# W_down of a decoder layer as seven products of quarters, with the quarter sums formed behind gate and up

## The chip, the cores and the metric

One core of a Trainium2 chip runs the whole program. The metric is the device time of one execution in microseconds; lower is better. A core has a matrix engine (TensorE; PE in the rows, PEld its weight loads), VectorE (DVE), ScalarE (ACT), GpSimd (POOL) and SyncE (SP), which issues most of the transfers. Each engine takes its own instructions in order and waits for the others by semaphores. Tiles lie in SBUF, products come out in PSUM, inputs and outputs lie in device memory (DRAM).

## What is computed

One layer of a hybrid decoder over 512 tokens of 1024 features, in float32: a gated short convolution and a sparse attention, merged by gates, then a SwiGLU feed-forward part and a final RMSNorm. The end, where the change lies, is this:

```
    h = h + mix @ w_o                                      # mix: 512 x 1024
    n = rmsnorm(h, g_ffn)
    h = h + (silu(n @ w_gate) * (n @ w_up)) @ w_down       # 512x1024 @ 1024x2816, 512x2816 @ 2816x1024
    return rmsnorm(h, g_final)
```

## The kernel before

**Splitting.** A matmul of float32 is made of three: each operand is split into a rounded part H (type float32r) and a remainder L, and `mm` (lines 117 to 121) adds H*H, H*L and L*H into one PSUM bank. A weight chunk, 128 x 1024, goes through `wchunk` (line 105): `load` puts it into `raw` by a transfer on SyncE's queue, `split` (line 92) copies it on ScalarE into `wh` (line 95) and subtracts on VectorE or GpSimd into `wl` (line 96). The pool `wp` has three buffers of each. In the matmul rows the names behind the arrow are the moving operand, then the stationary one.

**Order.** TensorE's instructions stand in the order of the source (`manual_schedule`); those of the other engines are put in order by a scheduler. Transfers on one queue are issued in their order, and one that waits holds up those behind it.

**Stages.** Projections, compressed keys, and an attention over 32 units with other products as filler take the first 430 us, with the output projection of the attention and W_o behind them until 526 us. Then, in `trace`:

- *Gate and up* (lines 909 to 936). For each of 22 feature tiles (`FT`) of 128 rows, `dense` multiplies a chunk of W_gate, then one of W_up, with the normalised tokens nH/nL (moving, 512 columns, 24 matmuls each). `ffn_act` (line 918) makes the activation: silu on ScalarE, the product on VectorE (line 921), then the split into `aH` and `aL` (lines 922, 923). The first three chunks are split early, into parts of aH/aL that are still free (`early_chunk`, line 857).
- *W_down* (lines 938 to 1009). Stationary is the activation, moving the chunk of W_down. First the left 512 output columns for all four token tiles, chunk by chunk, then the right 512, whose last token tile is cut into two halves of 256 columns. `wd_mm` is the inner product:

```
        for ff in range(2):
            k = 2 * fc + ff
            c = slice(ff * 512 + c0, ff * 512 + c0 + n)
            mm(ps, (aH[:, k, ts_], aL[:, k, ts_]), (w[0][:, c], w[1][:, c]),
               k == 0, k == FT - 1)
...
    for fc in range(NF):
        w = wchunk(a["wd"][0, fc], eng=nc.vector)
        for t in range(NT):
            wd_mm(pss[t], w, fc, t, 0, 512)
```

- *The end* (`add_sq`, `var`, `scale_out`, lines 946 to 1010). The PSUM tile is added into the residual `h1`, squared with a row sum on ScalarE, made into a power -0.5 on GpSimd; then `h1` is scaled and written out per token tile.

**Addresses.** SBUF tiles are placed one behind the other at multiples of 32 bytes. In the built program nH, nL, wh and wl begin at multiples of 128 bytes, aH and aL 96 bytes past one, yH and yL 32 past, oH, oL, q, th and tl 64 past.

Of the kernel before, what the change touches and what calls it, by code (L numbers as in the profile page):

```python
# [51 lines left out]
def trace(tc, a):  # L52
# [12 lines left out]
    gmix = const([P, KD], "gmix")  # L65
    convw = const([P, 4, 3], "convw")
# [453 lines left out]
    def expo(u, h):  # L520
        pr, i = units[u]
        if h == 0:
            U[u]["sm"] = ap_.tile([P, 2, 3], F32, name="sm", bufs=3)
        pt, nm = U[u]["pts"][h], U[u]["nms"][h]
        for b in range(3):
            s = U[u]["pc"][:, h] if b == 0 else pt[:, (b - 1) * S:(b - 1) * S + U[u]["w"]]
            nc.scalar.activation(s, s, AF.Exp,  # L527
                                 scale=-1.0, bias=nm[:, b:b + 1],
                                 accum_out=U[u]["sm"][:, h, b:b + 1])

    def norm(u):
        pr, i = units[u]
        fac = ap_.tile([P, 2, 3], F32, name="fac")
# [383 lines left out]

    def ffn_act(ft, pg, pu):
        sg = fp.tile([P, S], F32, name="sg", bufs=2)
        nc.scalar.activation(sg, pg, AF.Silu)  # L920
        nc.vector.tensor_tensor(sg, pu, sg, op=ALU.mult)  # L921
        nc.scalar.activation(aH[:, ft], sg, AF.Copy)
        nc.vector.tensor_tensor(aL[:, ft], sg, f(aH[:, ft]), op=ALU.subtract)

    ffn_act(0, pp[0], pp[1])
    for ft in range(1, FT):
        if ft == 1:
# [8 lines left out]
        ffn_act(ft, pg, pu)  # L936

    def wd_mm(ps, w, fc, t, c0, n):
        ts_ = slice(t * P, (t + 1) * P)
        for ff in range(2):  # L940
            k = 2 * fc + ff
            c = slice(ff * 512 + c0, ff * 512 + c0 + n)
            mm(ps, (aH[:, k, ts_], aL[:, k, ts_]), (w[0][:, c], w[1][:, c]),
               k == 0, k == FT - 1)

    def add_sq(ps, t, cs, q):
        nc.vector.tensor_tensor(h1[:, t, cs], ps, h1[:, t, cs], op=ALU.add)
# [9 lines left out]
    NF = FT // 2  # L957
    half = slice(0, 512)
    pss = [acc.tile([P, S], F32, name="acc") for _ in range(NT)]
    for fc in range(NF):  # L960
        w = wchunk(a["wd"][0, fc], eng=nc.vector)
        for t in range(NT):
            wd_mm(pss[t], w, fc, t, 0, 512)
    for t in range(NT):
        add_sq(pss[t], t, half, 0)
        var(t, 0, EPS)
        nc.gpsimd.tensor_tensor(h1[:, t, half], h1[:, t, half], gfin[:, half], op=ALU.mult)  # L967


    parts = [(t, 0, 512) for t in range(3)] + [(3, 0, 256), (3, 256, 256)]  # L970
    pss = [acc.tile([P, S], F32, name="acc") for _ in parts]

    def part(i, ws, f0):
        t, c0, n = parts[i]
        for q, w in enumerate(ws):
            wd_mm(pss[i][:, 0:n], w, f0 + q, t, c0, n)

    for fc in range(NF - 2):
        w = wchunk(a["wd"][1, fc], eng=nc.vector)
        for i in range(5 if fc < NF - 3 else 3):  # L980
            part(i, [w], fc)
    ws = [w] + [wchunk(a["wd"][1, fc], eng=nc.vector) for fc in range(NF - 2, NF)]

    rest = slice(512, D)

    def scale_out(t):
        r = st[:, t, 1:2]
        lo, hi = h1[:, t, half], h1[:, t, rest]
# [4 lines left out]
        (nc.scalar if t == 0 else nc.sync).dma_start(a["out_0"][t][:, half], lo)
        nc.vector.scalar_tensor_tensor(hi, in0=hi, scalar=r, in1=gfin[:, rest],
                                       op0=ALU.mult, op1=ALU.mult)
        nc.sync.dma_start(a["out_0"][t][:, rest], hi)

    for i, (t, c0, n) in enumerate(parts):
        if i < 3:
            part(i, ws[1:], NF - 2)  # L1000
        else:
            part(i, ws, NF - 3)
        q = 1 if i < 4 else 2
        add_sq(pss[i][:, 0:n], t, slice(512 + c0, 512 + c0 + n), q)
        if i in (1, 2, 4):
            scale_out(t - 1)
        var(t, q, st[:, t, 0:1])
        if i != 3:
            nc.gpsimd.tensor_tensor(st[:, t, 1:2], st[:, t, 0:1], mhalf[:, 0:1], op=ALU.pow)
    scale_out(3)  # L1010
# [3 lines left out]
def layout(inp):  # L1014
# [69 lines left out]
```

## Time and profile before

| | us |
|---|---|
| median of three runs (913.68 to 916.31) | 913.7 |
| the profiled execution | 913.92 |
| its span, first to last instruction | 912.1 |
| gate and up | 547.8 to 781.2 |
| W_down | 781.2 to 905.0 |
| after the last matmul | 7.1 |

The rows further down are of the profiled execution. Times in them count from its first instruction. A matmul's row lasts until its result is out, longer than the distance to the next one: how fast they follow each other is read from their starts. "Idle before" is the time that the engine stood still, with what ended it.

### The profile page before, as it was taken

The numbers are of one execution on the slowest core, as the hardware profiler recorded it, in microseconds if no ns is written. First come the engines' busy times: TensorE is split into PE (matmuls) and PEld (weight loads), VectorE is DVE, ScalarE is ACT, GpSimd is POOL, SyncE is SP. The second block draws the span as 40 slices with busy tenths as digits, with TensorE's granted clock in tenths as the row PEclk, the third lists the DMA queues.
The fourth block names the chain that finished last, engine by engine and source line by source line (L and its number), as shares of the span: only waits on it lengthen the run. The fifth ranks groups of instructions, "written<-read, shape, count | busy, mean of one in ns | idle before, by whom it ended". The sixth has DMA issues, their size and how long they took to land.

```text
span 912.1 us, 12767 instructions
## 1 busy us (share of the span) xinstructions
PE 892.1 (98%) x4757; PEld 761.3 (83%) x4757; DVE 518.0 (57%) x1219; ACT 425.0 (47%) x936; POOL 119.1 (13%) x79
## 2 busy tenths in 40 slices
PE   8989899999999999999999999999999999999996
PEld 7789788888888888888889999888888888888885
DVE  4896788888888888765456442333333333223223
ACT  6345686767767777664323522222233222212212
POOL 1000423233242222330000300000000000001100
PEclk9999999999999999999999999999999999999999
DMA  8235511211212121124434700233333233323312
GB/s 308 76 114 157 173 47 47 57 61 48 69 47 71 46 64 54 58 65 163 154 93 131 216 2 24 93 93 101 106 94 93 93 98 108 94 93 93 93 47 92
DMA packets 26269, 85.14 MB, mean 93 GB/s; under 512 B 3424, under 2 KB 3680, under 8 KB 26208
## 3 DMA queue, kind: packets, MB, share of 16 engines
q1 hardware_dynamic: 24912, 82.78, 28.9%
q10 hardware_dynamic: 1296, 1.55, 0.5%
q8 instruction: 37, 0.61, 0.3%
q14 instruction: 24, 0.20, 0.1%
HBM read 82.23 MB, written 2.10 MB: 92 GB/s over the span
## 4 chain that ended last, share of the span: by engine, by line
PE 89%; DVE 6%; ACT 3%; issue 1%; DMA 1%; POOL 0%; POOLq 0%; ACTq 0%; DVEq 0%
PE acc L119 24%; PE acc L120 24%; PE acc L121 24%; PE sc L500 4%; PE tp L568 4%; PE av L587 2%; PE av L586 2%; DVE blk L249 2%; PE sc L119 1%; PE sc L121 1%; PE sc L120 1%; ACT wh L95 1%; PE av L581 1%; DVE wl L96 1%; DMA raw<-wq 1%
## 5 line engine op out<-in xcount | busy, mean ns | idle before, releaser
L95 ACT ACTIVATE wh<-raw 128x1024 fp32r<-128x1024 f32 (+2 forms) x143 | 144.5, 1012 | 317.4 <-PE acc L120 116.0
L119 PE MATMUL acc<-nH,wh 128*128 128x512 f32 x656 | 262.7, 400 | 0.0
L121 PE MATMUL acc<-nH,wl 128*128 128x512 f32 x656 | 256.4, 391 | 1.1 <-POOL wl L96 1.1
L120 PE MATMUL acc<-nL,wh 128*128 128x512 f32 x656 | 256.3, 391 | 0.0
L96 DVE TENSOR_TENSOR wl<-raw,wh 128x1024 fp32r<-128x1024 f32 (+2 forms) x107 | 123.8, 1158 | 170.2 <-ACT wh L95 169.9
L121 PEld LDWEIGHTS acc<-nH,wl 128*128 128x128 f32 x656 | 123.2, 188 | 27.7 <-POOL wl L96 1.5
L119 PEld LDWEIGHTS acc<-nH,wh 128*128 128x128 f32 x656 | 123.5, 188 | 21.4
L120 PEld LDWEIGHTS acc<-nL,wh 128*128 128x128 f32 x656 | 123.6, 188 | 21.3
L96 POOL TENSOR_TENSOR wl<-raw,wh 128x1024 fp32r<-128x1024 f32 x36 | 86.2, 2399 | 232.9 <-ACT wh L95 91.1
L121 PE MATMUL acc<-wh,aL 128*128 128x512 f32 (+1 forms) x198 | 73.5, 371 | 0.0
L119 PE MATMUL acc<-wh,aH 128*128 128x512 f32 (+1 forms) x198 | 73.4, 371 | 0.0
L120 PE MATMUL acc<-wl,aH 128*128 128x512 f32 (+1 forms) x198 | 73.4, 371 | 0.0
L527 ACT ACTIVATE pt<-pt,nm 128x128 f32<-128x128 f32 (+3 forms) x128 | 70.7, 554 | 3.6 <-DVE nm L512 2.9
L512 DVE CUSTOM_DVE_ANT_0 pt<-sc,tri,nrs 128x128 f32<-128x128 f32 (+3 forms) x128 | 65.4, 547 | 0.1
L572 DVE TENSOR_TENSOR tl<-tp,th 128x512 fp32r<-128x512 f32 x80 | 55.2, 690 | 11.6 <-ACT th L571 9.8
L921 DVE TENSOR_TENSOR sg<-acc,sg 128x512 f32<-128x512 f32 x22 | 15.2, 692 | 80.7 <-PE acc L121 80.7
L571 ACT ACTIVATE th<-tp 128x512 fp32r<-128x512 f32 x80 | 47.3, 592 | 10.2 <-PE tp L568 9.3
L568 PE MATMUL tp<-ident,pt 128*128 128x128 f32 x320 | 48.3, 273 | 0.1
L967 POOL TENSOR_TENSOR h<-h,gfin 128x512 f32<-128x512 f32 x4 | 6.0, 1536 | 299.1 <-ACT jk L949 299.1
L120 PEld LDWEIGHTS acc<-wl,aH 128*128 128x128 f32 x198 | 37.3, 189 | 7.1
L119 PEld LDWEIGHTS acc<-wh,aH 128*128 128x128 f32 x198 | 37.3, 189 | 7.1
L121 PEld LDWEIGHTS acc<-wh,aL 128*128 128x128 f32 x198 | 37.3, 188 | 7.0
(231 smaller groups left out, 1503.8 us busy)
## 6 DMA issues: line engine op xcount, KB each, us to landing
raw<-wg SPq DMA_DIRECT2D x22, 512.0 KB, 3.5
raw<-wu SPq DMA_DIRECT2D x22, 512.0 KB, 3.5
raw<-wd SPq DMA_DIRECT2D x22, 512.0 KB, 3.5
raw<-wcv SPq DMA_DIRECT2D x12, 512.0 KB, 3.5
raw<-wq SPq DMA_DIRECT2D x8, 512.0 KB, 3.5
raw<-w SPq DMA_DIRECT2D x8, 512.0 KB, 3.5
raw<-wgc SPq DMA_DIRECT2D x8, 512.0 KB, 3.5
raw<-wga SPq DMA_DIRECT2D x8, 512.0 KB, 3.4
```

Source lines behind the costliest of these rows:

```text
L95: nc.scalar.activation(h[:, :n], raw[:, :n], AF.Copy)
L96: ins = (eng or nc.gpsimd).tensor_tensor(l[:, :n], raw[:, :n], f(h[:, :n]), op=ALU.subtract)
L119: nc.tensor.matmul(ps, lhs[0], rhs[0], start=first, stop=False)
L120: nc.tensor.matmul(ps, lhs[0], rhs[1], start=False, stop=False)
L121: nc.tensor.matmul(ps, lhs[1], rhs[0], start=False, stop=last)
L249: nc.vector.tensor_tensor(blk[lp * HD:(lp + 1) * HD, :, 2 * ct + hp, 0:NB - 1], src, pos, op=ALU.add)
L500: nc.tensor.matmul(o, q[:, h, qs], kk[g // 2][:, g % 2, c0:c0 + n], start=(j == 0), stop=(j == 1))
L512: nc.vector.tensor_tensor_reduce(out=pt[:, r0:r0 + w].rearrange("p (j c) -> p j c", c=P), in0=sv[:, b], in1=tri[:, NT - 1 - i:NT], scale=n ...
L527: nc.scalar.activation(s, s, AF.Exp, scale=-1.0, bias=nm[:, b:b + 1], accum_out=U[u]["sm"][:, h, b:b + 1])
L568: nc.tensor.transpose(tp[:, (2 * b + h) * P:(2 * b + h + 1) * P], pts[h][:, r0:r0 + P], ident)
L571: nc.scalar.activation(th, tp, AF.Copy)
L572: nc.vector.tensor_tensor(tl, tp, f(th), op=ALU.subtract)
```

## The change

With the activation A (512 x 2816) and W_down each cut into 2 x 2 quarters (256 x 1408 and 1408 x 512), the four quarters of the result come from seven products of quarters in place of eight; the operands of most are sums or differences of quarters. Row tiles: 2 per product, inner tiles: 11 (`NK`), 512 columns.

- *Weight sums.* Five sums or differences of quarters of W_down are formed once per inner tile, during feature tiles 2 to 12 of gate and up: `sums_load` fetches four pieces of 128 x 512 into the staging tiles of name `n2`, `sums` makes five results on VectorE (tied behind the newest activation product by a dependency for the scheduler) and writes them to a DRAM tile `scr`. Loads and stores are all on SyncE's queue.
- *Activations.* `ffn_act` now keeps the product in `a_`, in full, and for the first 11 feature tiles splits the operands of products 0 and 1 at once into `aC`, which has two slots. `prep_a` makes the operand of product i + 1 while product i runs, a difference of two quarters first where one is needed.
- *The product stage.* 42 chunks (six per product, the sixth of half width) are loaded three ahead, from `scr` or `wd`, into the `raw`, `wh` and `wl` buffers in turn. From the fourth on their split parts go into quarter slots of nH and nL, which then are the moving operands. Each product's two PSUM tiles are added to, or subtracted from, one or two quarters of `h1`. Token tiles 2 and 3 are complete after product 5 and written out then; the last product, in two halves of 256 columns for its second row tile, completes tiles 0 and 1.
- *Early chunks* get a pool of their own (`eyp`) for H, and parts of `aC` for L.
- *Even addresses.* Small constants share the tiles `few` and `rfew`; `uu`, `ssq` and `st` are padded; `sm` and `fac` get four buffers. In the built program nH, nL, wh, wl, a_, aC, yH, yL, oH, oL, q, th and tl all begin at multiples of 128 bytes.

The core of the diff:

```diff
-    gmix = const([P, KD], "gmix")
-    convw = const([P, 4, 3], "convw")
+
+    few = const([P, 32], "few")
+    gmix, rstd, warm = few[:, 0:8], few[:, 8:12], few[:, 12:13]
+    rfew = pool(es, name="rbase", bufs=1, side="right").tile([P, 24], F32, name="rfew")
+    convw = rfew[:, 0:12].rearrange("p (m j) -> p m j", j=3)
+    mhalf, nrs8, nrs = [rfew[:, i:i + NT] for i in (12, 16, 20)]
...
-            u = oyp.tile([P, S + 2], F32, name="uu")
+            u = oyp.tile([P, S + 32], F32, name="uu")[:, 0:S + 2]
...
-    aH = fp.tile([P, FT, S], F32R, name="aH")
-    aL = fp.tile([P, FT, S], F32R, name="aL")
+
+    NK = FT // 2
+    eyst = ExitStack()
+    eyp = pool(eyst, name="eyp", bufs=1, side="right", reuse_waits="tile")
+    aC = fp.tile([P, 2, 2, NK, 256], F32R, name="aC")
+    aCf = aC.rearrange("p s e k c -> p (s e k c)")
     early = []
 
     def early_chunk(src, eng):
         q = len(early)
-        r = slice(FT - 2 * q - 2, FT - 2 * q)
         raw = load(src, 1024)
-        h, l = [t[:, r].rearrange("p f s -> p (f s)") for t in (aH, aL)]
+        h = eyp.tile([P, 1024], F32R, name=f"ey{q}")
+        l = aCf[:, (10 - q) * 1024:(11 - q) * 1024]
...
         sg = fp.tile([P, S], F32, name="sg", bufs=2)
         nc.scalar.activation(sg, pg, AF.Silu)
-        nc.vector.tensor_tensor(sg, pu, sg, op=ALU.mult)
-        nc.scalar.activation(aH[:, ft], sg, AF.Copy)
-        nc.vector.tensor_tensor(aL[:, ft], sg, f(aH[:, ft]), op=ALU.subtract)
+        a = a_[:, ft]
+        ins = nc.vector.tensor_tensor(a, pu, sg, op=ALU.mult)
+        prods.append((ins.ins if hasattr(ins, "ins") else ins).name)
+        if ft < NK:
+            part_a(0, ft, 1, a[:, lo])
+            d = fp.tile([P, S], F32, name="sg", bufs=2)[:, lo]
+            nc.vector.tensor_tensor(d, a[:, hi], a[:, lo], op=ALU.subtract)
+            part_a(1, ft, 1, d)
+
+    def part_a(s, k, n, src):
+        h, l = [aC[:, s, e, k:k + n].rearrange("p k c -> p (k c)") for e in range(2)]
+        nc.scalar.activation(h, src, AF.Copy)
+        nc.vector.tensor_tensor(l, src, f(h), op=ALU.subtract)
...
+    def sums_load(k):
+        for i in range(4):
+            nc.sync.dma_start(quart[i], a["wd"][i // 2, i % 2][:, k * 512:(k + 1) * 512])
+
+    def sums(k):
+        cs = slice(k * 512, (k + 1) * 512)
+        o = [gffn[:, 0:512], gffn[:, 512:D]]
+        b11, b12, b21, b22 = quart
+        for n, out, x, y in (("11+12", o[0], b11, b12), ("12+22", b12, b12, b22),
+                             ("11-22", o[1], b11, b22), ("11+21", b11, b11, b21),
+                             ("21+22", b22, b21, b22)):
+            ins = nc.vector.tensor_tensor(out, x, y,
+                                          op=ALU.subtract if "-" in n else ALU.add)
+
+            tc.add_manual_dep(ins.ins if hasattr(ins, "ins") else ins, prods[-1],
+                              mybir.DependencyInfo(mybir.DependencyClass.Sync,
+                                                   mybir.DependencyReason.SCHED_ONLY))
+            nc.sync.dma_start(scr[SUMS[n]][:, cs], out)
...
+        if 2 <= ft < 2 + NK:
+            sums_load(ft - 2)
...
+    PRODS = [((0, 0), None, "12+22", [(0, 1, 1), (1, 1, 1)]),
+             ((1, 0), (0, 0), "11+12", [(1, 1, 1)]),
+             ((1, 1), (1, 0), "11", [(1, 0, -1), (1, 1, 1)]),
+             ((0, 1), (0, 0), "22", [(0, 1, 1), (0, 0, -1)]),
+             ((0, 0), (1, 1), "11-22", [(0, 0, 1), (1, 1, 1)]),
+             ((1, 1), None, "11+21", [(0, 0, 1), (1, 0, 1)]),
+             ((0, 1), (1, 1), "21+22", [(0, 0, 1)])]
+    NQ = (NK + 1) // 2
+    chunks = [(i, q) for i in range(len(PRODS)) for q in range(NQ)]
+    wq_ = {}
+
+    def prep_w(n):
+        if n >= len(chunks):
+            return
+        i, q = chunks[n]
+        b = PRODS[i][2]
+        w = 512 * min(2, NK - 2 * q)
+        src = scr[SUMS[b]] if b in SUMS else a["wd"][int(b[0]) - 1, int(b[1]) - 1]
+        src = src[:, q * 1024:q * 1024 + w]
+        if n < 3:
+            wq_[n] = wchunk(src, w, nc.vector)
+            return
+        nm = ("raw", "wh", "wl")[n % 3]
+        raw = wp.tile([P, 1024], F32 if nm == "raw" else F32R, name=nm)
+        raw = raw if nm == "raw" else f(raw)
+        nc.sync.dma_start(raw[:, :w], src)
+        r = slice(2 * (n % 4), 2 * (n % 4) + 2)
+        h, l = [t[:, r].rearrange("p k c -> p (k c)") for t in (nH, nL)]
+        nc.scalar.activation(h[:, :w], raw[:, :w], AF.Copy)
+        nc.vector.tensor_tensor(l[:, :w], raw[:, :w], f(h[:, :w]), op=ALU.subtract)
+        wq_[n] = h, l
...
+        k, n = 4 * piece, min(4, NK - 4 * piece)
+        (r, g), m = PRODS[i][0], PRODS[i][1]
+        x = a_[:, g * NK + k:g * NK + k + n, TH[r]]
+        if m is not None:
+            d = fp.tile([P, D], F32, name="n2", bufs=2)[:, 0:n * 256]
+            d = d.rearrange("p (k c) -> p k c", c=256)
+            nc.vector.tensor_tensor(d, x, a_[:, m[1] * NK + k:m[1] * NK + k + n, TH[m[0]]],
+                                    op=ALU.subtract)
+            x = d
+        h, l = [aC[:, i % 2, e, k:k + n] for e in range(2)]
+        nc.scalar.activation(h, x, AF.Copy)
+        nc.vector.tensor_tensor(l, x, f(h), op=ALU.subtract)
...
+    AHEAD = 3
+    for n in range(AHEAD):
+        prep_w(n)
+    for i in range(len(PRODS)):
+        last = i == len(PRODS) - 1
+        pss = [acc.tile([P, S], F32, name="acc") for _ in (PARTS if last else PARTS2)]
+        for q in range(NQ - 3 if last else NQ):
+            n = i * NQ + q
+            prep_w(n + AHEAD)
+            for ps, (u, c0, c1, _) in zip(pss, PARTS if last else PARTS2):
+                wd_mm(ps, n, u, c0, c1)
+            if q % 2:
+                prep_a(i + 1, q // 2)
+        if last:
+            break
+        for u in range(2):
+            for r, c, sign in PRODS[i][3]:
+                evac(pss[u], u, r, c, sign)
...
+            elif i == 5:
+                square(2 + u, CH[0], 1)
+                var(2 + u, 1, st[:, 2 + u, 0:1])
+                rpow(2 + u)
+                scale_out(2 + u)
+
+    for ps, (u, c0, c1, q) in zip(pss, PARTS):
+        for n in range(len(chunks) - 3, len(chunks)):
+            wd_mm(ps, n, u, c0, c1)
```

**Two places where the order changes.** First SyncE's queue in gate and up; `raw` is a weight chunk's buffer, n_6071 and n_6072 are the two staging tiles, gffn holds two of the five results. Before, pairs of wg and wu follow each other with nothing between them, up to the last pair, the chunks of W_down and the outputs:

```order
L89 DMA raw<-wg 128x1024
L89 DMA raw<-wu 128x1024
L89 DMA raw<-wd 128x1024 x22
L996 DMA out<-h_5317 128x512
L993 DMA out<-h_5317 128x512
```

With the change, from one pair in the middle of gate and up to the next:

```order
L88 DMA raw<-wg 128x1024
L88 DMA raw<-wu 128x1024
L973 DMA scr<-gffn 128x512 x2
L973 DMA scr<-n_6071 128x512 x2
L973 DMA scr<-n_6072 128x512
L958 DMA n_6072<-wd 128x512
L958 DMA n_6071<-wd 128x512 x2
L958 DMA n_6072<-wd 128x512
L88 DMA raw<-wg 128x1024
L88 DMA raw<-wu 128x1024
```

Between two pairs of weight chunks there now stand five stores of sums and four loads of the next pieces.

Second VectorE in the W_down stage. Before, from the end of gate and up through the left half of the output (line 96 the splits of weight chunks, line 947 the additions into h1):

```order
L921 TENSOR_TENSOR sg<-acc,sg 128x512
L96 TENSOR_TENSOR wl<-raw,wh 128x1024
L923 TENSOR_TENSOR aL<-sg,aH 128x512
L96 TENSOR_TENSOR wl<-raw,wh 128x1024 x10
L947 TENSOR_TENSOR h_5317<-acc,h_5317 128x512 x2
L954 TENSOR_SCALAR st<-ssq 128x1
```

With the change, between the additions of product 1 and those of product 2 (line 1034 makes differences of activation quarters, n_7950 to n_8216; line 1039 their remainders; line 1022 splits weight chunks):

```order
L1022 TENSOR_TENSOR nL<-raw,nH 128x1024
L1022 TENSOR_TENSOR nL<-wh,nH 128x1024
L1039 TENSOR_TENSOR aC<-n_7950,aC 128x768
L1022 TENSOR_TENSOR nL<-wl,nH 128x512
L1039 TENSOR_TENSOR aC<-n_7992,aC 128x1024
L1034 TENSOR_TENSOR n_8028<-a 128x1024
L1034 TENSOR_TENSOR n_8058<-a 128x768
L1022 TENSOR_TENSOR nL<-raw,nH 128x1024
L1039 TENSOR_TENSOR aC<-n_8028,aC 128x1024
L1022 TENSOR_TENSOR nL<-wh,nH 128x1024
L1034 TENSOR_TENSOR n_8216<-a 128x1024
L1022 TENSOR_TENSOR nL<-wl,nH 128x1024
```

Where splits of weight chunks stood alone, they now alternate with differences and remainders of activations.

## Rows read from the trace of the kernel before

**Rows 1.** The page: busy time per engine, and the chain that ended last.

```profile
PE 892.1 (98%) x4757; PEld 761.3 (83%) x4757; DVE 518.0 (57%) x1219; ACT 425.0 (47%) x936; POOL 119.1 (13%) x79
...
PE 89%; DVE 6%; ACT 3%; issue 1%; DMA 1%; POOL 0%; POOLq 0%; ACTq 0%; DVEq 0%
```

**Rows 2.** Windows: length, busy time and count per engine, granted clock, DMA share, GB/s.

```profile
547.80:781.20 233.40, 233.40 (x1074) 195.17 (x1073) 76.86 (x83) 66.18 (x85) 0.00 (x0) 1.00 0.30 91
781.20:905.00 123.80, 123.77 (x594) 102.47 (x593) 34.77 (x41) 28.18 (x39) 7.64 (x7) 1.00 0.26 81
905.00:912.10 7.10, 0.00 (x0) 0.00 (x0) 1.65 (x5) 1.34 (x5) 0.54 (x1) 0.83 0.39 148
```

**Rows 3.** Timeline, TensorE, gate and up, then W_down: start, us, engine, line, operation.

```profile
600.14 0.39 PE L119 MATMUL acc<-nH,wh 128*128 128x512 f32 x1
...
700.11 0.39 PE L119 MATMUL acc<-nH,wh 128*128 128x512 f32 x1
...
781.03 0.39 PE L119 MATMUL acc<-wh,aH 128*128 128x512 f32 x1
...
847.09 0.28 PE L119 MATMUL acc<-wh,aH 128*128 128x256 f32 x1
...
848.50 0.40 PE L119 MATMUL acc<-wh,aH 128*128 128x512 f32 x1
```

**Rows 4.** Timeline, TensorE: six matmuls with oH/oL, ten of W_o with nH/nL.

```profile
459.86 0.39 PE L119 MATMUL acc<-oH,wh 128*128 128x512 f32 x1
...
461.24 0.39 PE L119 MATMUL acc<-oH,wh 128*128 128x512 f32 x1
...
493.97 0.28 PE L119 MATMUL acc<-wh,nH 128*128 128x256 f32 x1
...
495.17 0.28 PE L120 MATMUL acc<-wl,nH 128*128 128x256 f32 x1
```

**Rows 5.** Groups of instructions by form, VectorE and ScalarE: busy us, mean ns, idle before.

```profile
L96 DVE TENSOR_TENSOR wl<-raw,wh 128x1024 fp32r<-128x1024 f32 x91 | 112.5, 1236 | 167.4 <-ACT wh L95 167.2
...
L96 DVE TENSOR_TENSOR wl<-raw,wh 128x512 fp32r<-128x512 f32 x8 | 5.5, 686 | 0.9 <-ACT wh L95 0.9
...
L947 DVE TENSOR_TENSOR h<-acc,h 128x512 f32<-128x512 f32 x7 | 4.7, 687 | 5.7 <-PE acc L121 5.7
...
L947 DVE TENSOR_TENSOR h<-acc,h 128x256 f32<-128x256 f32 x2 | 0.8, 416 | 0.0
...
L95 ACT ACTIVATE wh<-raw 128x1024 fp32r<-128x1024 f32 x127 | 134.2, 1058 | 304.8 <-PE acc L120 108.7 <-issue 97.2 <-PE acc L121 81.2
```

**Rows 6.** DMA issues: KB each, us to landing; then xT's and out's landing.

```profile
raw<-wd SPq DMA_DIRECT2D x22, 512.0 KB, 3.5
...
xT<-xT SPq DMA_DIRECT2D x8, 256.0 KB, 4.5
...
DMA to landing us min/median/max: 2.7/4.5/6.6
...
DMA to landing us min/median/max: 2.0/2.3/2.8
```

**Rows 7.** Windows in which the DMA engines were full; the last figure is GB/s.

```profile
9.00:12.00 3.00, 3.00 (x15) 2.46 (x14) 1.20 (x2) 0.63 (x1) 0.00 (x0) 1.00 1.03 342
...
432.00:436.00 4.00, 4.00 (x20) 3.30 (x19) 2.82 (x4) 1.00 (x2) 0.00 (x0) 1.00 1.00 364
```

**Rows 8.** Timeline, VectorE, gate and up.

```profile
640.71 1.23 DVE L96 TENSOR_TENSOR wl<-raw,wh 128x1024 fp32r<-128x1024 f32 x1 [0.16 <-ACT wh L95]
...
646.14 1.23 DVE L96 TENSOR_TENSOR wl<-raw,wh 128x1024 fp32r<-128x1024 f32 x1 [3.61 <-ACT wh L95]
```

**Rows 9.** Timeline, the end: last matmul, last addition, last output.

```profile
904.70 0.28 PE L121 MATMUL acc<-wh,aL 128*128 128x256 f32 x1
...
905.27 0.41 DVE L947 TENSOR_TENSOR h<-acc,h 128x256 f32<-128x256 f32 x1
...
908.43 0.38 SPq L996 DMA_DIRECT2D out<-h  x1
```

More of the change, by code (lines that the diff above doesn't have):

```diff
@@ L532, in norm @@
         pr, i = units[u]
-        fac = ap_.tile([P, 2, 3], F32, name="fac")
+        fac = ap_.tile([P, 2, 3], F32, name="fac", bufs=4)
         gv = gates[:, i].rearrange("p (b h) -> p h b", h=HEADS)[:, 2 * pr:2 * pr + 2]
@@ L916, in trace @@
     dense(pp[2][:, hi], wgu[2], nH, nL, cols=hi)
+    FH = (slice(0, NK), slice(NK, FT))
+    TH = (lo, hi)
+    SUMS = {"12+22": 0, "11+12": 1, "11+21": 2, "11-22": 3, "21+22": 4}
+    sd = pool(es, name="sd", bufs=1, space=bass.MemoryType.DRAM)
+    scr = sd.tile([5, P, NK * 512], F32, name="scr")
+    eyst.close()
+    fq = pool(es, name="fq", bufs=1, side="right", reuse_waits="tile")
+    a_ = fq.tile([P, FT, S], F32, name="a")
     def ffn_act(ft, pg, pu):
@@ L936, in trace @@
         ffn_act(ft, pg, pu)
[L938 to L947, printed above, removed]
+        if 2 <= ft < 2 + NK:
+            sums(ft - 2)
@@ new lines, in prep_a @@
+    def prep_a(i, piece):
+        if not 2 <= i < len(PRODS):
+            return
+        k, n = 4 * piece, min(4, NK - 4 * piece)
[10 more added lines that the diff above has]
+        nc.vector.tensor_tensor(l, x, f(h), op=ALU.subtract)
@@ L948, in add_sq, with wd_mm, square @@
+    def wd_mm(ps, n, u, c0, c1):
+        i, q = chunks[n]
+        w = wq_[n]
+        for kk in range(min(2, NK - 2 * q)):
+            k = 2 * q + kk
+            at = [aC[:, i % 2, e, k, u * P:(u + 1) * P] for e in range(2)]
+            c = slice(kk * 512 + c0, kk * 512 + c1)
+            mm(ps[:, c0:c1], at, (w[0][:, c], w[1][:, c]), k == 0, k == NK - 1)
+    def square(t, cs, q):
         jk = lp.tile([P, S], F32, name="jk", bufs=2)
@@ L955, in var @@
                                 op0=ALU.mult, op1=ALU.add)
[L957 to L984, printed above, removed]
+    def rpow(t):
+        nc.gpsimd.tensor_tensor(st[:, t, 1:2], st[:, t, 0:1], mhalf[:, 0:1], op=ALU.pow)
@@ L995, in scale_out @@
+        nc.vector.scalar_tensor_tensor(y, in0=y, scalar=r, in1=gfin[:, CH[0]],
                                        op0=ALU.mult, op1=ALU.mult)
[L996 to L1009, printed above, removed]
@@ L1011, in trace @@
+    for ps, (u, c0, c1, q) in zip(pss, PARTS):
+        for n in range(len(chunks) - 3, len(chunks)):
+            wd_mm(ps, n, u, c0, c1)
+        cs = slice(c0, c1)
+        nc.vector.tensor_tensor(h1[:, u, cs], h1[:, u, cs], ps[:, cs], op=ALU.add)
+        square(u, cs, q)
+        if q == 1 and u == 1:
+            scale_out(0)
+        var(u, q, st[:, u, 0:1])
+        if (u, q) != (1, 1):
+            rpow(u)
+    scale_out(1)
     es.close()
```

50 lines of the change are left out of this document (32 added, 18 removed).

## The prediction

> **What bounds the kernel now.** First the page's busy shares and its chain of waits [rows 1]: TensorE is busy 98% of a 912.1 us span and holds 89% of the chain, so time is won only where TensorE has less to do or is fed sooner. The window table by stage [rows 2] then shows where this change works. Gate and up (547.8 to 781.2) keep TensorE busy without a gap with VectorE at 77 of 233 us and the DMA engines 30% busy at 91 GB/s; W_down (781.2 to 905.0) is 123.8 us of TensorE with VectorE at 35; a tail of 7.1 us follows in which TensorE does nothing. The granted clock is 1.00, the 2.4 GHz level, in both stages.
>
> How long a matmul takes is read from the distance of starts, since the durations of the rows overlap. In gate and up 441 matmuls of 512 columns lie between 600.14 and 700.11: 226.7 ns each. In W_down the 282 of 512 columns from 781.03 to 847.09 take 234.3 ns, the 12 half-width ones after them 117.5 [rows 3]. Nothing waits between them. The stage is 462 full and 132 half matmuls, 594 in the table's count, and 462 x 234.3 + 132 x 117.7 ns is its 123.8 us.
>
> **The change, part by part.**
>
> *The products.* Seven products of quarters, each 2 x 11 x 3 = 66 matmuls of 512 columns, are 462 in place of 528 full-width equivalents; as the order of the changed program shows, 429 stand at full width and 66 at half (the last product's second row tile). What each costs is the open point. The changed program moves nH/nL slices over stationary aC, both tiles at multiples of 128 bytes, where aH/aL began 96 bytes past one. Low end: the spacing of gate and up, whose moving operand is the same nH/nL: 429 x 226.7 + 66 x 113.3 = 104.7 us. High end: W_down's present spacing: 429 x 234.3 + 66 x 117.7 = 108.3 us. Rows do not say that the address decides: the products with oH start 64 bytes past a multiple of 128 and are spaced 230 ns, but W_o's first half has both operands at such multiples and is spaced 120.0 ns at 256 columns [rows 4], above the 113.3 that half of 226.7 would be. I take 230 ns, between the ends and equal to the oH row, and 116.5 for the halves: 98.7 + 7.7 = 106.4 us. **-17.4 us**, ends -15.5 and -19.1.
>
> By the Trainium skill (TensorE: Matmul & The Clock Gate, Back-to-back issue gap) the warm spacing follows from the columns alone, 215.7 ns at 512. By it 66 fewer matmuls save 14.2 us (an estimate) and addresses nothing; both spacings of the trace lie above it, so I use the rows.
>
> *Other tiles at even addresses.* In the built program 96 products with yH/yL, 192 with oH/oL, 256 with q, 320 with th/tl and 144 of the first gate and up products had an operand off a multiple of 128: 1,008. At nothing each (the W_o rows) to about 4 ns (half of W_down's 7.6, most being narrower) that is 0 to -4.0 us; **-1.2 us**, near the W_o end, because attention also waits for other engines.
>
> *Weight chunks and row-block operands in the product stage.* Per chunk ScalarE has one copy of 1.06 us and VectorE one subtraction of 1.24; a half chunk 0.69 [rows 5]; I take a 768-wide one at 0.96, between them. Per product VectorE gets five chunks and a half chunk (6.9 us), the remainders of the next product's left operand (2 x 1.24 + 0.96 = 3.4), in four products their differences before that (3.4), and two or four additions into h1 at 0.69 (1.4 or 2.8). TensorE needs 66 x 0.230 = 15.2. Products 2 and 3 have everything: 16.5, so VectorE falls 1.3 us behind in each. Over the stage it has 44.4 + 17.2 + 11.3 + 15.1 = 88 us before the last product's own additions, against 106, and it may be up to three chunks of 2.8 us ahead, since four slots of nH/nL take turns. In product 0 the list is 14.3 and in product 1 15.1, so some lead survives. **+0.5 us**, ends 0 and +2.6 (no lead). Chunk 4 is the tightest load: its buffer is chunk 0's, free 2.8 us into the stage, and 3.5 to landing [rows 6] plus 1.06 and 1.24 makes 8.6, where TensorE wants it at 11.0. ScalarE's 8.9 us per product are covered.
>
> *Quarter sums.* Over eleven feature tiles of 10.9 us each (two products of 24 x 0.2267) come 5 additions of 0.69 on VectorE, 3.4 us, so its load is 0.69 + 3 x 0.42 + 2 x 1.24 + 3.4 = 7.8 of 10.9: covered. On SP come four loads and five stores of 256 KB per tile, and wg and wu of a later tile stand behind them: 11 issues of about 0.33 us. The loop that must close within 10.9 us runs from the last sum: its store 0.35 + 2.3 to landing, the load that takes its place 0.35 + 4.5 (xT's median, same size, taken while the engines were full), four sums 2.8: 10.3 us. By bytes a tile moves 1.05 of weights + 1.05 + 1.31 = 3.41 MB; full engines moved 342 to 364 GB/s [rows 7], so 9.4 to 10.0 us. Both fit, barely: **0**, at the upper ends a loss (rival B). The cover if they don't fit: a split may start when a weight buffer frees, two chunks (10.9 us) before its use, as the splits 5.43 us apart show [rows 8]; 2.3 of that is its own work, and sums that stand ahead of it on VectorE take some 1.3 more, so about 7 us of lag cost TensorE nothing.
>
> *The tail.* From the last matmul's start (904.70) to the end the same add, square, power and scaling follow [rows 9]; rows 256 to 511 leave a product earlier: 0, within 0.5. Tiles for constants, padding and two more buffers of sm and fac: nothing waited for them.
>
> **Sum.** -17.4 - 1.2 + 0.5 = -18.1 on the profiled execution's 913.9 us (its span and 1.8 around it): 895.8. The median of the runs is 0.2 lower: **895.6 us**.
>
> **Rivals.**
>
> A: *addresses change nothing.* Spacing stays 234.3: -15.5 + 0.5, so 898.7 us. For: W_o's rows. Against: gate and up run at 226.7 with the same moving tile. The skill's rule above is this case told more strictly and would give about 900.
>
> A': *both tiles do reach 226.7 and the other products profit*: -19.1 and up to -4.0, 890.6 to 893.
>
> B, *the other side: the quarter loop does not close.* SP takes its queue in order; if a store lands late, the load behind it, the sums, and then wg and wu all slip, and VectorE stands before a load with the next splits behind it. With a loop of L us the lag is 11 x (L - 10.9), less the 7 covered. At L = 12 TensorE loses 5 us (900.6), at L = 13.2 it loses 18 and the whole gain is gone: that is the turning point. The slowest rows, 2.8 for a store and 6.6 for a load, give 0.35 + 2.8 + 0.35 + 6.6 + 2.8 = 12.9, 15 us lost: 910.6. Against: those 6.6 were seen at the start, where several loads were issued at once. The skill (DMA: Bandwidth & Descriptors, Latency and other measured facts) has HBM access at 0.2 us on average and 2 under high load. With 1.8 more on each landing the loop would be about 13.9 (an estimate), some 26 us lost; this trace, with stores only at the end, cannot show it.
>
> C: *VectorE binds products 2 to 5* without any lead: +2.6, 897.7 us.
>
> D: *the change does not do what it says*: fewer matmuls are certain from the order (4,658 against 4,757), so this could only be that another wait takes their place at 781, at most 0.02.
>
> **How the numbers follow.** Forecast 0.38; A' 0.17; A 0.18; C 0.08; B between 11.6 and 13.2 us of loop 0.11; B beyond 0.06; D 0.02. A measurement of this kernel tells about 0.3%, 2.7 us, from no change. Everything but B's upper part and D is faster by more: 0.92. Same 0.02 (B close to its turning point or D), slower 0.06. The range goes from A' to B at a loop of 12.2: 890.5 to 903; left out are 0.04 below, and above it B's rest, 0.14.
>
> **What would show it.** Right: 4,658 matmuls; TensorE without gaps from 547 to the end of the products; the stage some 106 us; spacing of acc<-nH,aC between 226.7 and 234.3, which settles A, A' and the forecast by itself; DMA in gate and up near 300 GB/s with VectorE 70% busy until the thirteenth tile. Wrong: TensorE idle before gate and up products released by wl's subtraction or a load (B), or idle inside products 2 to 5 released by VectorE's nL or aC (C); a distance of the sums above 10.9 us in gate and up (B).

## The result and the profile after

The changed kernel takes **897.5 us** (median of four runs, 896.9 to 898.8) where the kernel before took 914.1 beside it: ratio 0.9816, 95% interval 0.980 to 0.9832. Forecast were 895.6, within 890.5 to 903. The profiled execution has a span of 895.9 us, 16.2 less than before.

The page of the changed kernel, busy time and chain, against [rows 1]:

```profile
PE 875.3 (98%) x4658; PEld 746.5 (83%) x4658; DVE 607.9 (68%) x1349; ACT 451.0 (50%) x970; POOL 118.3 (13%) x77
...
PE 85%; DVE 7%; ACT 3%; DMA 2%; issue 1%; SPq 0%; POOL 0%; POOLq 0%; ACTq 0%; DVEq 0%
```

TensorE is still busy 98%, with 4,658 matmuls; VectorE has gone from 57 to 68%. The windows of gate and up, of the products and of the tail (columns as in [rows 2]):

```profile
548.20:781.50 233.30, 233.30 (x1073) 194.92 (x1072) 110.83 (x152) 62.86 (x86) 0.00 (x0) 1.00 0.60 200
781.50:889.10 107.60, 107.60 (x496) 88.56 (x494) 89.35 (x102) 58.02 (x72) 6.71 (x5) 1.00 0.53 174
889.10:895.90 6.80, 0.07 (x1) 0.00 (x0) 1.51 (x4) 1.31 (x4) 0.54 (x1) 0.83 0.40 154
```

Gate and up take the 233.3 us that they took, though VectorE's time rose from 77 to 111 and the traffic from 91 to 200 GB/s. The products take 107.6 in place of 123.8, TensorE never idle in them. That is nearly all: from the first product's start to the last one's start 107.42 us against 123.67 (-16.25); the first product starts 0.45 later (781.48 against 781.03); from the last start to the end 6.97 in place of 7.41 (-0.44). Together -16.24.

The timeline of TensorE gives the spacing in the new stage; between these two rows lie 308 matmuls of 512 columns:

```profile
796.82 0.39 PE L118 MATMUL acc<-nH,aC 128*128 128x512 f32 x1
...
868.39 0.39 PE L120 MATMUL acc<-nH,aC 128*128 128x512 f32 x1
```

71.57 us / 308 = **232.4 ns**. [Rows 3] have 234.3 in W_down and 226.7 in gate and up; 230 was forecast. The starts repeat every 21 matmuls to the nanosecond (228 to 241 ns). Rows have whole nanoseconds; but for 1 to 2 ns it is every 7, as in W_down before, while in gate and up nearly every distance is 226 or 227 ns. A PSUM tile takes six matmuls of a chunk, and 7 fits no buffer's turn here. That speaks for the stream of operands itself as what sets the spacing; the first experiments test it.

The quarter sums did not run as forecast. VectorE's timeline around the last of the eleven, and the product that needs the split behind it:

```profile
684.62 1.23 DVE L95 TENSOR_TENSOR wl<-raw,wh 128x1024 fp32r<-128x1024 f32 x1
691.82 0.69 DVE L967 TENSOR_TENSOR gffn<-n 128x512 f32<-128x512 f32 x1 [5.98 <-DMA n<-wd]
...
694.85 1.22 DVE L95 TENSOR_TENSOR wl<-raw,wh 128x1024 fp32r<-128x1024 f32 x1
...
700.32 0.39 PE L120 MATMUL acc<-nH,wl 128*128 128x512 f32 x1
```

VectorE stands 6 us before a load of a quarter, and the split behind the sums is done at 696.07, 4.26 us before its use. When the sums are over, this lead is 9.04: a split at 733.58 ends at 734.80 and is used at 743.84. From the second feature tile with sums on, the first additions start at 588.77, 599.66, 610.54, 621.41, 632.29, 643.17 (10.88 apart, TensorE's pace), then at 654.46, 665.64, 678.68 and 691.82: 11.3, 11.2, 13.0 and 13.1 apart, 5.1 us behind in the end. The page has the median landing times behind it:

```profile
n<-wd SPq DMA_DIRECT2D x44, 256.0 KB, 3.7
scr<-n SPq DMA_DIRECT2D x33, 256.0 KB, 4.2
...
scr<-gffn SPq DMA_DIRECT2D x22, 256.0 KB, 4.3
```

### The profile page after: what moved, and what is told of

It reads as the page before. It is cut to its first block, busy times and chain, and to the rows that moved or that the text cites. A ratio compares the mean times of both kernels' runs of the same rounds, so it can differ in the third digit from the quotient of the medians.

```text
span 895.9 us, 12997 instructions
## 1 busy us (share of the span) xinstructions
PE 875.3 (98%) x4658; PEld 746.5 (83%) x4658; DVE 607.9 (68%) x1349; ACT 451.0 (50%) x970; POOL 118.3 (13%) x77
## 4 chain that ended last, share of the span: by engine, by line
PE 85%; DVE 7%; ACT 3%; DMA 2%; issue 1%; SPq 0%; POOL 0%; POOLq 0%; ACTq 0%; DVEq 0%
PE acc L118 23%; PE acc L120 23%; PE acc L119 23%; PE sc L499 4%; PE tp L567 4%; PE av L586 2%; PE av L585 2%; DVE blk L248 2%; DVE wl L95 1%; ACT wh L94 1%; PE av L580 1%; DMA w2kr<-w2k 1%; DMA raw<-wk 1%; DMA xT<-xT 0%; DMA xt<-x 0%
## 5 line engine op out<-in xcount | busy, mean ns | idle before, releaser
L94 ACT ACTIVATE wh<-raw 128x1024 fp32r<-128x1024 f32 (+2 forms) x124 | 124.3, 1005 | 239.2 <-PE acc L119 188.6
L95 DVE TENSOR_TENSOR wl<-raw,wh 128x1024 fp32r<-128x1024 f32 (+2 forms) x88 | 100.0, 1138 | 53.2 <-ACT wh L94 52.3
L120 PE MATMUL acc<-nH,aC 128*128 128x512 f32 (+1 forms) x201 | 71.4, 355 | 0.0
L511 DVE CUSTOM_DVE_ANT_0 pt<-sc,tri,rfew 128x128 f32<-128x128 f32 (+3 forms) x128 | 65.4, 545 | 0.1
L938 DVE TENSOR_TENSOR a<-acc,sg 128x512 f32<-128x512 f32 x22 | 15.2, 691 | 70.2 <-PE acc L120 60.4
L119 PE MATMUL acc<-nL,aC 128*128 128x512 f32 (+1 forms) x153 | 57.9, 378 | 0.0
L118 PE MATMUL acc<-nH,aC 128*128 128x512 f32 (+1 forms) x153 | 57.9, 378 | 0.0
L570 ACT ACTIVATE th<-tp 128x512 fp32r<-128x512 f32 x80 | 47.3, 592 | 10.3 <-PE tp L567 9.5
L526 ACT ACTIVATE pc<-pc,nm 128x32 f32<-128x32 f32 x64 | 20.5, 320 | 47.1 <-DVE nm L506 46.9
L1108 POOL TENSOR_TENSOR h<-h,gfin 128x512 f32<-128x512 f32 x2 | 3.4, 1701 | 302.5 <-ACT jk L1052 302.5
L542 DVE TENSOR_SCALAR pt<-pt,fac 128x128 f32<-128x128 f32 (+3 forms) x128 | 42.8, 379 | 0.0
L120 PEld LDWEIGHTS acc<-nH,aC 128*128 128x128 f32 x201 | 37.8, 188 | 5.8
```

The lines of the kernel that those rows point to most:

```text
L94: nc.scalar.activation(h[:, :n], raw[:, :n], AF.Copy)
L95: ins = (eng or nc.gpsimd).tensor_tensor(l[:, :n], raw[:, :n], f(h[:, :n]), op=ALU.subtract)
L118: nc.tensor.matmul(ps, lhs[0], rhs[0], start=first, stop=False)
L119: nc.tensor.matmul(ps, lhs[0], rhs[1], start=False, stop=False)
L120: nc.tensor.matmul(ps, lhs[1], rhs[0], start=False, stop=last)
L511: nc.vector.tensor_tensor_reduce(out=pt[:, r0:r0 + w].rearrange("p (j c) -> p j c", c=P), in0=sv[:, b], in1=tri[:, NT - 1 - i:NT], scale=n ...
```

## The experiments

Three questions were open: what sets the spacing, what the sums cost and how near they are to binding, and how near VectorE is. Medians are beside the kernel before on the same chip, whose median was 915.9 us for the first group of runs, 914.5 for the second and 915.6 for the third, so ratios count rather than microseconds. Stage lengths and spacings agree between profiles of the same stage within 0.01 us and 0.1 ns (107.42 us in five of them), so the stages carry the argument and the whole times only go along with it.

**What sets the spacing.** In the built program nH, nL, wh and wl begin at the same place modulo 512 bytes, before and after; aC begins 384 past them, aH and aL began 352 past. The first group moves aC, with the tiles `ey` and `a_` that lie below it; in the product stage aC is the only matmul operand of these:

```
-    aC = fp.tile([P, 2, 2, NK, 256], F32R, name="aC")
-    aCf = aC.rearrange("p s e k c -> p (s e k c)")
+    aCf = fp.tile([P, 4 * NK * 256 + PAD], F32R, name="aC")[:, 0:4 * NK * 256]
+    aC = aCf.rearrange("p (s e k c) -> p s e k c", s=2, e=2, k=NK)
```

with PAD 96, 32, 8 and, later, 16; a larger PAD puts aC lower by four bytes for each element.

*aC 0 past (PAD 96).* 

> The changed kernel with aC (and ey and a_ below it) 384 bytes lower, so that aC begins at a multiple of 512 bytes as nH, nL, wh and wl do; nothing else is moved. In the changed kernel aC begins 384 past such a multiple, and its products stand 232.4 ns apart, with a strict period of 21 matmuls. Theory (distance): what sets the spacing is the distance of the stationary operand's address from the moving one's, modulo 256 or 512; at 0 (gate and up: 226.7 ns) it is shortest. Then 226.7 at 512 columns, the stage 429 x 0.2267 + 66 x 0.119 = 105.1 us in place of 107.4, the kernel 895.1 us. Rival 1 (multiples of 128 are all that counts): 232.4 as now, 897.5. Rival 2 (the order of the stage, six matmuls to a PSUM tile and then the next, sets it): 232.4 as now, 897.5.

*aC 256 past (PAD 32).* 

> The same with aC 128 bytes lower than in the changed kernel: 256 past a multiple of 512. The products with oH in the changed kernel stand so to wh and are spaced 226.7. Theory (distance, modulo 256): 226.7 ns, stage 105.1 us, kernel 895.1. Distance modulo 512: anything between 226.7 and 234.3. Rivals 1 and 2: 232.4 and 897.5.

*aC 352 past (PAD 8).* 

> The same with aC 32 bytes lower than in the changed kernel: 352 past a multiple of 512, the distance that aH had from wh before the change (and 96 past a multiple of 128). Theory (distance): 234.3 ns with a period of 7 matmuls, as before; stage 429 x 0.2343 + 66 x 0.1185 = 108.3 us, kernel 898.4. Rival 1 (multiples of 128): 234.3 too, the same time. Rival 2 (order of the stage): 232.4, 897.5.

The same 308 matmuls in the timelines, of ac_off0:

```profile
797.83 0.39 PE L118 MATMUL acc<-nH,aC 128*128 128x512 f32 x1
...
867.64 0.39 PE L120 MATMUL acc<-nH,aC 128*128 128x512 f32 x1
```

of ac_off352:

```profile
797.96 0.40 PE L118 MATMUL acc<-nH,aC 128*128 128x512 f32 x1
...
870.12 0.40 PE L120 MATMUL acc<-nH,aC 128*128 128x512 f32 x1
```

69.81 / 308 = 226.7 ns, the stage 105.09 us; and 72.16 / 308 = 234.3 ns with a period of 7, the stage 108.17. ac_off256 has 226.7 and 105.09 as well. In whole times: 896.7 (ratio 0.9796, 0.9782 to 0.9809), 896.8 (0.979, 0.9777 to 0.9803) and 899.1 (0.9824, 0.9803 to 0.9846). Expected were 895.1, 895.1 and 898.4; the kernel before ran 1.8 us longer beside these than beside the changed kernel. Moving the stationary tile by 32 to 384 bytes, with no instruction changed, carries the stage to both of the spacings known from other stages. Rival 2 falls with all three. Rival 1 falls with ac_off0 and ac_off256: 0, 256 and 384 are all multiples of 128 and do not give the same. What counts is the distance of the two operands modulo 256. That it is the distance, and not the place of the stationary operand by itself, follows from W_down before: there the built program has the moving chunk 128 and the stationary tile 480 past a multiple of 512, in ac_off352 they are 0 and 352 past, and the spacing (234.3 ns) and the period (7) are the same. Modulo 256 rather than 512 is shown at one pair, 0 and 256.

*The kernel before with the padding alone.* 

> The kernel before with the change's padding alone (constants in one tile, sm and fac with four buffers, uu, ssq and st longer): all matmul operands at multiples of 128 bytes, aH and aL 384 past a multiple of 512, W_down as it was. By the prediction the other tiles are worth -1.2 us and W_down's 462 full and 132 half products at 230 and 116.5 ns 121.6 us in place of 123.8: 910.5 in all. Theory (distance): 232.4 ns in W_down, 123.0 us, -0.8; oH's 192 products 2.4 ns less, -0.5; the rest as in the changed kernel, where nothing else got faster: 912.8. Rival 2 (order of the stage): W_down unchanged, 913.6.

Edit: gmix, rstd and warm into one tile `few`, the other small constants into `rfew`, sm and fac with four buffers, uu, ssq and st longer, as in the change. W_down's first 264 matmuls lie between these rows:

```profile
782.64 0.40 PE L117 MATMUL acc<-wh,aH 128*128 128x512 f32 x1
...
843.99 0.39 PE L117 MATMUL acc<-wh,aH 128*128 128x512 f32 x1
```

They are 232.4 ns apart with the period of 21, as in the changed kernel with quite another order of products: 122.91 us from first to last start, -0.76. The products with oH and oL take 226.7 in place of 229.0. In all 914.2, ratio 0.9983 (0.9974 to 0.9992), -1.6 us; -1.2 of it is seen in these two places.

*The kernel before with aH and aL at 0.* 

> The kernel before with the change's padding and with aH and aL at multiples of 512 bytes, W_down still as 594 products: it takes the address out of the comparison. Theory (distance): W_down at 226.7 and 119.6 ns, 462 x 0.2267 + 132 x 0.1196 = 120.5 us in place of 123.8, kernel 910 where the kernel before has 913.7; the seven products, at the same distance 105.1, are then worth 15.4 us by themselves. Rival (spacing in W_down has other causes as well): 122.9 us or more.

Edit: before_even with `aL = fp.tile([P, FT * S + 96], ...)`, which lowers both. Two rows of its timeline, 264 matmuls apart:

```profile
782.57 0.39 PE L117 MATMUL acc<-wh,aH 128*128 128x512 f32 x1
...
842.41 0.39 PE L117 MATMUL acc<-wh,aH 128*128 128x512 f32 x1
```

226.7 ns; W_down 120.59 us from first to last start; 913.3, ratio 0.9972 (0.9961 to 0.9983), so -2.6 us (-3.6 to -1.6) where -3.7 was expected, while the stage alone is 3.08 shorter. Against ac_off0's 105.09 the seven products are worth **15.5 us** when the distance is 0 in both: the 33 full and 66 half matmuls fewer, 33 x 0.2267 + 66 x 0.1195 = 15.4. The other 0.75 us of the 16.25 come from the distance, 96 modulo 256 for aH and 128 for aC.

*Distance 64.* 

> The changed kernel with aC 64 bytes lower: 320 past a multiple of 512, so that the stationary operand begins 64 past the moving one modulo 256. The one long row of this distance is in the kernel before, wh moved over bh at 256 columns: 113.3 ns, less than the 120.0 of distance 0. Theory (a step of 16 columns in place of 32 at this distance): 220 ns at 512 columns and 113.3 at 256, stage 101.9 us, kernel 892. Rival (distances other than 0 modulo 256 all lie between 229 and 235 at 512 columns, as 96, 128, 192 and 224 do): stage 106 to 108.5, kernel 897 to 899.

The theory of a smaller step fell: 796.71 to 868.57 for the 308, 233.3 ns with a period of six (two, but for the rounding of the rows); the stage 107.61; 897.8 us, ratio 0.9814 (0.9797 to 0.9831). At half width the spacing is 115.8 on average, the lowest seen in this stage, and at distance 0 it is 119.5, the highest: what is best at 512 columns is not best at 256.

At 256 columns the distance does not fix the spacing alone. Two stretches of products with early chunks in this run, all at distance 64, of 46 and 94 distances:

```profile
540.73 0.28 PE L119 MATMUL acc<-nL,ey 128*128 128x256 f32 x1
...
545.94 0.28 PE L120 MATMUL acc<-nH,aC 128*128 128x256 f32 x1
...
547.05 0.28 PE L119 MATMUL acc<-nL,ey 128*128 128x256 f32 x1
...
558.12 0.28 PE L120 MATMUL acc<-nH,aC 128*128 128x256 f32 x1
```

The first has 113.3 ns, the second 117.8. What else counts there is open.

**The sums.** *Left out.* 

> The changed kernel without the quarter sums: no loads, additions and stores for them; the five products that take a sum read the quarter W11, W12 or W21 itself instead, so the values are other ones and the matmuls, splits and their loads the same. It measures what the sums cost. The prediction (0; lag covered) and the trace of the changed kernel (the sums fall 5.1 us behind, the smallest lead of a split over its matmul is 4.3 us): no difference, 897.5, and TensorE without a gap as now. Rival (the traffic of the sums also slows TensorE or the loads): 896 or less.

Edit: no calls of sums_load and sums, and `src = a["wd"][...]` in prep_w for all seven products. The windows from the first av<-gh,VC matmul to the first product, of no_sums:

```profile
114.16:779.60 665.44, 663.88 (x3588) 568.08 (x3589) 398.21 (x1035) 326.87 (x771) 96.50 (x50) 1.00 0.25 83
```

and of the changed kernel:

```profile
116.02:781.48 665.46, 663.92 (x3589) 567.89 (x3590) 431.52 (x1090) 326.69 (x771) 96.45 (x50) 1.00 0.38 122
```

665.44 against 665.46 us, with 33 us of VectorE more: 55 additions, 44 loads and 55 stores cost TensorE nothing. The stage itself has 232.4 ns in both. The whole time, 897.1 us (0.9805, 0.9787 to 0.9822), cannot be told from the changed kernel's; of its profile's 2.0 us shorter span 1.9 arise before that first matmul.

*Stores doubled.* 

> The changed kernel with each stored sum stored a second time into DRAM that nobody reads: ten stores a feature tile, 4.72 MB a tile in place of 3.41. It tests where rival B begins. If bytes bind the loop: at 342 to 364 GB/s 13.0 to 13.8 us a tile against 10.9, a lag of about 25 us over eleven tiles, of which the lead of 9 us covers a part: TensorE loses some 16 us in gate and up before matmuls that wait for wl, kernel 913. If the loop still has room: 897.5 to 899.

Edit: after each store of a sum a second one into another DRAM tile. TensorE's waits between 600 and 740 us:

```profile
PE acc L118 <- ACT wh L94: 31.6, 6, 7.3
PE acc L120 <- DVE wl L95: 2.4, 1, 2.4
```

943.4 us, ratio 1.0324 (1.029 to 1.0358): slower than before by 29, and some 46 above the changed kernel, three times what was expected. The sums are 11 to 27 us apart. The chain that ended last shows how one round goes (its longer pieces):

```profile
635.28 0.58 SPq L974
635.90 3.36 DMA scr<-n
639.65 6.55 DMA raw<-wu
646.22 1.07 ACT wh L94
647.33 0.80 PE acc L118
648.13 0.43 PE acc L119
```

The loads of the next quarters wait for a store to land, wu stands behind them on SP, and the activation product behind wu releases the next sums by the tie. So once a sum is later than the lead, each delay makes the next. Bytes alone do not bind: the DMA engines are 78% busy from 600 to 660, where TensorE waits, and 96% from 660 to 690, where it does not. And TensorE, having waited, starts its matmuls 0.43 us apart, as at the 1.2 GHz level; the window from 600 to 660 has a mean granted clock of 0.80 (columns as in [rows 2]):

```profile
600.00:660.00 60.00, 42.70 (x147) 32.37 (x147) 24.31 (x37) 11.60 (x16) 0.00 (x0) 0.80 0.78 272
660.00:690.00 30.00, 30.00 (x134) 24.87 (x133) 18.15 (x27) 7.69 (x12) 0.00 (x0) 1.00 0.96 334
```

Waits are 34 us of a delay of 52 in the profiled execution (the first product starts at 833.3 in place of 781.5); the rest, 18 us, are matmuls that follow each other more slowly, most of them at 0.43 us. The linear count by bytes had neither this chain on SP nor the clock.

**VectorE.** *AHEAD at 1.* 

> The changed kernel with AHEAD at 1 in place of 3: each chunk of the product stage is prepared one chunk before its use, so the lead that covers VectorE's additions and remainders is gone. The trace of the changed kernel has splits ready 3.5 to 5 us before use; two chunks are 5.6 us. Theory (the lead covered VectorE): TensorE waits before chunks behind the additions, one or two waits of 0.5 to 2 us in each of six products, 4 to 12 us, kernel 902 to 910. Rival (VectorE has room without the lead, or the order was set by buffers and not by AHEAD): 897.5.

Edit: `AHEAD = 1`, with the last two chunks prepared before the last product's final part. 897.2 us (0.9805, 0.9788 to 0.9822), the stage 107.42 as before. The theory fell, but in a weak test: the order in which VectorE gets its work hardly changed, since it follows from buffers that come free and not from the number. Splits behind the additions are ready 1.9 us before use in place of 4.3 to 4.5, and one in the last product 0.7 in place of 2.6. That is less than a chunk's 2.8 us, and it is still enough.

*Remainders twice.* 

> The changed kernel with each of the twelve remainders of the left operand in the product stage formed twice on VectorE: 13.6 us more, 103 of the stage's 107. It tests rival C. VectorE has 13.9 to 15.1 us in each of products 1 to 4 where TensorE needs 15.4, and splits that are 3.5 to 5 us ahead; with 2.3 to 3.4 more in a product it falls behind by 1 to 3 us in each, some 8 over four, so TensorE waits about 4 to 5 us before matmuls that want nL or aC: kernel 902. If the lead is larger than the splits show (work can be taken from product 0, 5 and 6): 897.5 to 898.5.

Edit: the subtraction into aC in prep_a written twice. There are fifteen such remainders and not twelve, and VectorE is busy 105.6 us in the stage in place of 89.3, so 16.2 more and not 13.6. TensorE's waits in this stage, from the table of waits:

```profile
PE acc L119 <- DVE nL L1022: 4.3, 3, 2.0
```

The stage is 112.46 us, +5.04, which is about the 4 to 5 us expected, but not where they were: three matmuls that want nL start 2.2, 1.6 and 1.0 us late, all at the last three chunks of the last product, and none before. 903.3 us (0.9863, 0.9838 to 0.9887), beside 898.3 for the changed kernel on the same chip. So of the 16.2 us added 11.2 went unnoticed, and 5 did not: VectorE is covered, with less to spare over the stage than its idle 18 us suggest.

**The version that the runs point to.** *Base.* 

> The changed kernel once more, unaltered, as the base of the two that follow on the same chip: 897.5 us, product stage 107.4 us at 232.4 ns.

*All long runs at distance 0.* 

> The changed kernel with aC 384 bytes lower, as in ac_off0, and fac's buffers padded so that yH, yL and the probabilities pt begin at multiples of 256 too: every long run of 512-column products then has its two operands at distance 0 modulo 256. Theory (distance): product stage 105.1, -2.3 us; the 96 products with yH/yL 226.7 in place of 232, -0.5 us; 2.3 to 2.8 us below the unaltered changed kernel of this call. Rival (the time of the rest moves by as much for other reasons): within 1 us of it.

Edit: PAD 96 and `fac = ap_.tile([P, 16], F32, name="fac", bufs=4)[:, 0:6]`. 896.6 us (895.3 to 897.7; ratio 0.979, 0.9775 to 0.9806) beside 898.3 (898.0 to 898.5; 0.9809, 0.9795 to 0.9823). No run of the one reaches the other, though the intervals of the ratios overlap. The stage is 105.09 against 107.42; the same 308 matmuls, 226.7 ns apart:

```profile
796.46 0.39 PE L118 MATMUL acc<-nH,aC 128*128 128x512 f32 x1
...
866.28 0.39 PE L120 MATMUL acc<-nH,aC 128*128 128x512 f32 x1
```

yL's products stand 227 ns apart in place of 231 (medians), and the stretch from the first product with yH to the first with oH is 0.3 us shorter. Against that, the early chunks at 256 columns now also stand at distance 0, and from the first product with oH to the first of the seven it is 333.38 us in place of 333.00. In these runs it is faster than both kernels, by 1.7 us than the changed one, less than the 2.3 to 2.8 expected and more than the rival's 1.

## Why the prediction was right, step by step

**The products: -17.4 forecast, -16.25 measured.** Matmuls fewer were counted right (429 full and 66 half). The spacing was 232.4 and 118.5 ns where I took 230 and 116.5; 429 x 0.2324 + 66 x 0.1185 = 107.5 us. Mis-sized by 1.1 us, within the ends given. The thought behind 230, that both tiles at multiples of 128 bytes would bring aC some of the way to gate and up's 226.7, was wrong: that needs a distance of 0 modulo 256. The padding took the stage's distance from 96 to 128, worth 1.9 ns of the 7.6; that this lands near the 230 is luck.

The 226.7 of gate and up and W_o's 120.0 at 256 columns [rows 4], the second of which I read as speaking against addresses, are both distance 0. Seen as columns at 2.4 GHz they are 32 columns above 512 and above 256. Distance 0 has the shortest spacing at full width and among the longest at half width, which hid the rule.

By the Trainium skill (TensorE: Matmul & The Clock Gate, Back-to-back issue gap) a single matmul's warm gap follows from the columns N alone, N / 2.4 + 2.5 ns, which makes 215.8 ns at 512 and 14.2 us for 66 matmuls fewer (both estimates). No stream here reaches that, the best being 226.7, and the same columns take 226.7 to 234.3. By the same page of the Trainium skill (Step-by-step: what each phase is for) the array has two independent read ports for the moving operand and the weight load, so that loading the next weights takes no read bandwidth from the running matmul. The spacing here depends on the distance of just these two addresses, which such ports by themselves do not account for; no run shows how it arises.

**Other tiles at even addresses: -1.2 forecast, +0.45 in the profile.** The reason failed: multiples of 128 bytes make nothing faster by themselves. Of the 1,008 products only the 192 with oH and oL gained clearly, 0.44 us (43.96 to 43.52 from the first of them to W_o), since their distance went from 192 to 0 modulo 256. yH's went from 235 to 232 (medians); those with q, th and tl kept 231 to 235 ns at 512 columns and 118 at 256. Half of q's are at distance 0 now and still take 231 ns at 512 columns: they come in short groups between other shapes, and the rule is shown for long runs alone. The 1,008 had left out W_o's second half, 192 products that went from 119.9 to 118.7 ns, and the 96 of the first stage with bh, which became slower (113.3 to 119.5 at 256 columns, distance 64 to 0).

From the first av<-gh,VC matmul to the first product it is 665.46 us after and 665.99 before, so -0.5. The start of the program took back more: that matmul starts at 116.02 in place of 115.04. The waits up to there differ from run to run, and the first product starts between 779.6 and 783.6 us over the thirteen profiles in which gate and up do not wait, at 781.5 and 782.2 in two of the same kernel. So the +0.45 is no effect that a single profile can show. In whole times before_even leaves -0.8 us beside the -0.76 of its W_down, with an interval from -1.6 to 0: neither 0 nor -1.2 is ruled out.

**VectorE in the products: +0.5 forecast, 0 measured.** The stage is the sum of its spacings. Windows of products 1 to 4:

```profile
797.00:812.40 15.40, 15.40 (x68) 12.46 (x68) 15.09 (x17) 8.64 (x10) 0.00 (x0) 1.00 0.68 241
812.40:827.70 15.30, 15.30 (x67) 12.42 (x66) 13.90 (x15) 8.53 (x10) 0.00 (x0) 1.00 0.61 188
827.70:843.10 15.40, 15.40 (x68) 12.47 (x67) 13.96 (x17) 8.64 (x10) 0.00 (x0) 1.00 0.63 190
843.10:858.40 15.30, 15.30 (x67) 12.40 (x66) 14.07 (x17) 9.77 (x14) 3.40 (x2) 1.00 0.62 188
```

VectorE is busy 89 us in the stage, and in none of these products longer than TensorE's 15.3 to 15.4, where I had 16.5 for products 2 and 3. I had added up the lengths of rows, and rows that follow each other directly overlap by some 0.1 us, as these two of 1.22:

```profile
783.68 2.35 DVE L1022 TENSOR_TENSOR nL<-raw,nH 128x1024 fp32r<-128x1024 f32 x2
```

Over the stage the rows add up to 95.8 us, in 89.3 busy. The tightest is chunk 4 (counted from 0), as forecast: nL ends at 791.48, used at 792.86, 1.4 us where I had 2.4. rem_twice shows C's mechanism with 16 us more on VectorE, and then in the last product and not in 2 to 5.

**Quarter sums: 0 forecast, 0 measured, for a reason half wrong.** The loop was priced at 10.3 us with a store's landing at 2.3, from stores of a quiet stretch, and a load's at 4.5; they were 4.2 and 3.7 under load, so 0.35 + 4.2 + 0.35 + 3.7 + 2.8 = 11.4, and the last two rounds took 13.1. That is B's sign (above 10.9), and the last two rounds lie in B's range (11.6 to 13.2). It cost nothing because the slip came only in the last four rounds, 5.1 us in all, and the lead that covers it is 9.0 and not 7. That the rounds ended before the lead did is in part luck. The warning that it fits barely was right; sums_twice is rival B, and dearer than its line, which gives some 20 us for a loop of 13.4 where 46 were lost.

**The tail: 0 forecast, -0.44 measured,** at the edge of what was allowed.

The errors, +1.1 and +1.6 on the first two, -0.5 and -0.4 on VectorE and the tail, left 1.9 us of the 18.1; that they cancelled by 0.9 is luck. The count of matmuls and the cover of the sums carried the forecast; its account of addresses did not.

## What to carry to other kernels

Take the distance of starts of a stream that nothing interrupts, and look whether it repeats: a period that fits no buffer's turn points to the operands themselves, and an address may then be moved to test it, here for 2 to 3% of a stage. For long runs of float32r products with 512 columns lay the moving and the stationary tile at the same place modulo 256 bytes, and measure at other widths. Extra traffic in a stage that TensorE bounds was free here up to the lead of what it stands before, so read that lead; beyond it the loss was not linear, since a queue that is served in order turns one late store into a late weight, and waiting costs the clock too.

## What was not expected of the hardware

Distance of stationary from moving operand modulo 256 bytes, with the spacing in long runs at 512 columns: 0: 226.7 ns (gate and up, oH after the change, the products of ac_off0, W_down of before_off0); 64: 233.3; 96: 234.3; 128: 232.4; 192: 229.0 (oH before). At 256 columns: 0: 119.5 to 120.0; 64: 113.3 (bh before) to 117.8 (ac_off320); 96: 117.4 to 118.8; 128: about 118.5. Neither the traffic nor VectorE beside it changes the first of these: gate and up have 226.7 over 441 matmuls at 91 GB/s before, and as much in the changed kernel, where the last figure of this window is 301 GB/s:

```profile
600.00:630.00 30.00, 30.00 (x134) 24.85 (x133) 18.86 (x29) 9.22 (x13) 0.00 (x0) 1.00 0.89 301
```

Why the distance counts, why the starts repeat as they do (every matmul at distance 0, every second at 64, every seventh at 96 and 128, but for the rounding of the rows), and what else sets the spacing at 256 columns, was not settled.
